# The convolution's diagonals behind the last norm's root in GpSimd's queue, and the lower parts of 5 routing chunks instead of 12 on GpSimd

## The chip, the cores and the metric

The program runs on one core of one Trainium2 chip. The metric is device time in microseconds (us), the median of several runs. "The profile" is one execution recorded by the hardware profiler.

## The reference

Three blocks run one after the other on 256 tokens of width 1024, in float32: an attention layer with a product-key expert network (PEER), a block with a conformer convolution and a recurrent mixer between feed-forward layers, and a block with sliding-window attention. The change touches the PEER network and the convolution:

```python
def peer_ffn(h, w_q, sub_k1, sub_k2, expert_u, expert_v):
    q = (ht @ w_q).reshape(T, 8, 256)
    s1 = einsum('thd,nd->thn', q[..., :128], sub_k1)       # 128 scores per head and half
    s2 = einsum('thd,nd->thn', q[..., 128:], sub_k2)
    v1, i1 = top_k(s1, 16);  v2, i2 = top_k(s2, 16)
    cand = v1[..., :, None] + v2[..., None, :]             # 256 sums per head
    vals, pos = top_k(cand, 16)
    experts = i1 * 128 + i2, taken at pos
    gates = softmax(vals)
    w = gelu(x . expert_u[experts]) * gates
    return sum of w * expert_v[experts]

def conformer_conv_module(x, ...):                         # x is rms_norm of the residual
    a, gate = split(x @ w_in + b_in, 2)
    h = a * sigmoid(gate)
    h = causal depthwise convolution of width 31 of h, + b_dw
    return silu(layer_norm(h)) @ w_out + b_out
```

## The kernel before

**Weights.** Tokens are held as two tiles of 128 rows. Weights come from memory in chunks of 128 x 2048 float32 (1 MB), loaded by SyncE's queue into `raw`, which has three buffers. `stream` splits each chunk in two halves of 1024 columns: ScalarE rounds the high part `wh` (L107), and the lower part `wl` = `raw` - `wh` (L109) is made by VectorE, or by GpSimd where `pool` is true. TensorE multiplies three times: high by high (L125), high by the activations' lower part (L126), lower part by high (L127). `wh` and `wl` have three slots.

```python
eng = nc.gpsimd if pool else nc.vector
for i in range(2):
    nc.scalar.copy(h[:, c], r[:, c])
    eng.tensor_tensor(l[:, c], r[:, c], h[:, c].bitcast(F32), op=OP.subtract)
```

**The PEER network.** Since every expert can be chosen, `up` multiplies all of `peer_u` by the tokens (64 chunks, each with two results that ScalarE turns to `ga` by gelu, L1048), while `routing` finds the chosen experts on VectorE; `weave` alternates steps of the two. For each token tile `routing` forms `cand` (L951) and takes the top 16 of 8 heads (L920 to L923), then the gates: `g` = values minus the largest (L962), the exponent on ScalarE, `den`, `g` (L965 to L967). The positions are split in `xb` (L985). For each half (first key, second key) `ib` (L990) holds the key numbers as float16, `eq` (L993, L995, L997) picks the chosen ones, `idx` (L999) is their sum, which TensorE transposes (L1001). Later the chosen experts are written as one-hot products to memory, from where the down projection reads them. TensorE runs the chunks of `up` while VectorE does all that, and takes one chunk after the other; ScalarE holds `wh` of coming chunks, the exponent and `ga` in one queue. The lower parts of chunks 0 to 11 of `up` are GpSimd's.

**The convolution.** `pre_norm` makes the normed input `xn`: ScalarE squares two halves of the residual into sums (L151), GpSimd adds them (`va`, L155) and takes the root by a power (`ya`, L158) in `rstd`, VectorE multiplies (L173), TensorE transposes (L213), and ScalarE and VectorE split the result (`xx`, L120, L121). This is done for both token tiles, just behind the feed-forward layer before. `conv` then streams `conv_in` (8 chunks, gated to `hp`) and convolves by channel blocks of 128: blocks 0 to 3 and 8 taps of block 5 by chains of multiply-adds on VectorE (L1220, L1224), block 4 on ScalarE and GpSimd (L1240, L1243), blocks 6 and 7 and 23 taps of block 5 by TensorE: for each tap a product with a diagonal matrix (`pc`, L1265). The diagonals `dg` are made from the weights `wd` by 14 `affine_select` instructions on GpSimd (L1213), each of up to 7 taps (128 x 896). Behind the products come transposes (`pt`, L1276), a layer norm and `conv_out`.

**Order.** Each engine takes its instructions in the order of its queue. A scheduling framework lays this order out when the program is built; the code's order goes in, and `issue_after(x)` keeps an instruction behind `x`.

Of the kernel before, what the change touches and what calls it, by code (L numbers as in the profile page):

```python
# [15 lines left out]
OP = mybir.AluOpType  # L16
# [10 lines left out]
class Core:  # L27
# [117 lines left out]
    def rstd(self, parts, n, p=128):  # L145

        nc = self.nc
        ss = self.sm.tile([128, 2], F32, tag="ss", name="ss")[:p]
        for i, part in enumerate(parts):
            junk = self.wk.tile([128, 512], F32, tag="junk", name="junk")[:p, :part.shape[-1]]  # L150
            nc.scalar.activation(junk, part, AF.Square, scale=n ** -0.5, accum_out=ss[:, i:i + 1])  # L151
        v = self.sm.tile([128, 1], F32, tag="va", name="va")[:p]
        y = self.sm.tile([128, 1], F32, tag="ya", name="ya")[:p]
        if len(parts) == 2:
            nc.gpsimd.tensor_scalar(v, ss[:, 0:1], EPS, ss[:, 1:2], op0=OP.add, op1=OP.add)  # L155
        else:
            nc.gpsimd.tensor_scalar(v, ss[:, 0:1], EPS, None, op0=OP.add)
        nc.gpsimd.tensor_tensor(y, v, self.half[:p, 0:1], op=OP.pow)  # L158
        return y

    def halves(self, x, p=128):
# [724 lines left out]
class Peer:  # L886
# [153 lines left out]
    def up(self):  # L1040
        k, nc = self.k, self.k.nc
        for c in range(64):
            hl = k.stream(k.a["peer_u"][c], pool=c < 12)
            for i in range(2):
                ps = k.tp((128, S), tag="tq")
                k.linear_stat(hl, i, ps)
                g = self.pool.tile([128, S], F32, tag="ga", name="ga", bufs=self.AHEAD)
                nc.scalar.activation(g, ps, AF.Gelu_apprx_tanh)  # L1048
                self.ga[c * 2 + i] = g
            yield  # L1050

    def down(self, up):
        k, nc, pool = self.k, self.k.nc, self.rp
        acc = [[k.acc(name=f"o{t}{h}") for h in range(2)] for t in range(2)]
# [14 lines left out]
        for c in range(64):  # L1069
            if c % 4 == 0:  # L1070
                G = pool.tile([128, S // self.GRP, 8, self.GRP], F32, tag="g8", name="G", bufs=2)
                nc.scalar.dma_start(G, self.gd[:, :, c * 2:c * 2 + 8, :])
            for _ in range(1 if c else 5):
                next(up, None)
            vs = [x.rearrange("p (e h n) -> p e h n", e=2, h=2) for x in k.stream(k.a["peer_v"][c])]
            ws = []
            for i in range(2):
                e = c * 2 + i
                w = self.ga.pop(e)
                w3 = w.rearrange("p (a b) -> p a b", b=self.GRP)  # L1080
                nc.vector.tensor_tensor(w3, w3, G[:, :, e % 8, :], op=OP.mult)
                wh = pool.tile([128, S], F32R, tag="wth", name="wth", bufs=5)
                wl = pool.tile([128, S], F32R, tag="wtl", name="wtl", bufs=5)
                k.split(wh, wl, w)
                ws.append((wh, wl))
            if c < 62:
                for i in range(2):
                    part(c * 2 + i, vs, ws[i])
            else:
                last += [(c * 2 + i, vs, ws[i]) for i in range(2)]  # L1090
# [11 lines left out]
    def run(self):  # L1102
        up = self.up()
        done = [0]

        def n(i):
            x = i >= 7 if i < 20 else i % 5 in (0, 3)
            x = min(x, self.AHEAD // 2 - 5 - done[0])
            done[0] += max(x, 0)
            return max(x, 0)  # L1110
        with self.k.tc.tile_pool(name="route", bufs=1) as self.rp:
            weave(self.routing(), up, n)
        with ExitStack() as ctx:
            self.rp = ctx.enter_context(self.k.tc.tile_pool(name="down", bufs=1))
            self.k.work(ctx)
            self.down(up)
# [3 lines left out]
class Block2:  # L1120
# [68 lines left out]
    def conv(self):  # L1189
        k, nc, a = self.k, self.k.nc, self.k.a  # L1190
        with ExitStack() as ctx:
            k.temp(ctx, "cvt")
            pool = ctx.enter_context(k.tc.tile_pool(name="cv", bufs=1))
            tl = lambda n, sh, dt=F32: pool.tile(sh, dt, name=n)
            par, wd = tl("par", [128, 3, 8]), tl("wd", [128, 8, 31])
# [9 lines left out]
            y = hp[:, :, 30:]  # L1205
            ysum, y5 = tl("ysum", [128, S]), tl("y5", [128, S])
            diag = {cb: tl(f"dg{cb}", [128, n, 128]) for cb, n in ((7, 31), (6, 31), (5, first))}
            for cb in (5, 6, 7):
                n = diag[cb].shape[1]
                for w in range(0, n, 7):  # L1210
                    d = diag[cb][:, w:min(w + 7, n)]
                    m = d.shape[1]
                    nc.gpsimd.affine_select(d, wd[:, cb, w:w + m, None].to_broadcast([128, m, 128]), pattern=[[0, m], [-1, 128]],  # L1213
                                            base=0, channel_multiplier=1, compare_op=OP.is_equal, fill=0.0)
            tap = lambda cb, w: hp[:, cb, w:w + S]
            chains = []

# [239 lines left out]
class Block3:  # L1457
# [267 lines left out]
    def mix(self, l, nt):  # L1725
        k, nc, a = self.k, self.k.nc, self.k.a
        with ExitStack() as ctx:
# [16 lines left out]
            def attention():  # L1744
                flush()
                for t in (2, 0, 1)[3 - nt:]:
                    yield from self.attention(l, t, sink, ga)
            side, conv = attention(), self.conv(l, nt)
            weave(iter(lambda: next(conv, True), True), side, lambda i: 2)
            for _ in side:  # L1750
                pass
# [226 lines left out]
```

## Time and profile before

| | |
|---|---|
| median of 3 runs | 2835.39 us (2831.9 to 2836.78) |
| the profiled execution | 2840.85 us, of which the span 2838.9 |
| mean granted TensorE clock | 0.981 of full speed |
| TensorE busy | 2726.2 us, 96% of the span |
| VectorE busy | 1851.3 us, 65% |
| ScalarE busy | 1417.2 us, 50% |
| GpSimd busy | 295.1 us, 10% |

PE is TensorE, DVE VectorE, ACT ScalarE, POOL GpSimd, SP SyncE. L109 is line 109 of the program; `wl<-raw,wh` names what an instruction writes and reads. A row in order of time gives start, duration, engine, line, operation, tiles, shapes and the number of instructions that it sums up; in brackets stands how long the engine stood idle before it, and whose work ended that. The routing stretch is that from 338 to 421 us, and the convolution's norm lies at 1304 to 1326 us.

### The profile page before, as it was taken

Reading aid. Unit: us, or ns where it says so; the run is one execution under the profiler, and the core shown is the slowest. Engines: PE = TensorE matmul, PEld = TensorE weight load, DVE = VectorE, ACT = ScalarE, POOL = GpSimd, SP = SyncE. Lnnn points to the kernel's source line nnn. Section 1 sums busy time; section 2 is a strip of 40 time slices with the busy share of each in tenths; the row PEclk is TensorE's granted clock in tenths of the full one; section 3 lists DMA queues with packets and bytes.
Section 4 is the critical chain, followed back from the end, with each engine's and each line's share of the span. In section 5 each row is a group of like instructions: output and inputs, shape, how many; then the busy total and the mean of one; then the engine's idle time right before and its main releaser. Section 6 shows DMA issues by size and latency. Waiting matters only on the chain.

```text
span 2838.9 us, 42369 instructions
## 1 busy us (share of the span) xinstructions
PE 2726.2 (96%) x16916; PEld 2423.5 (85%) x16916; DVE 1851.3 (65%) x3170; ACT 1417.2 (50%) x2454; POOL 295.1 (10%) x314
## 2 busy tenths in 40 slices
PE   7899979999999999999999999999999999999999
PEld 5787979989999887888888888897888878889897
DVE  6757698775555555766876576676766565466654
ACT  5544445544444555654556455524655454454543
POOL 2001650000000000002400000151001110000100
PEclk9899989999999999999999999999999999999999
DMA  5323436796665555554255465524554334433452
GB/s 208 146 103 140 145 125 249 287 314 220 208 216 202 191 193 205 193 191 167 76 199 193 170 215 188 195 90 155 195 192 158 121 115 156 163 131 123 162 193 104
DMA packets 105973, 496.58 MB, mean 175 GB/s; under 512 B 11040, under 2 KB 44320, under 8 KB 50224
## 3 DMA queue, kind: packets, MB, share of 16 engines
q1 hardware_dynamic: 61632, 443.15, 43.8%
q10 hardware_dynamic: 44144, 50.74, 5.4%
q8 instruction: 132, 2.16, 0.3%
q14 instruction: 65, 0.53, 0.1%
HBM read 476.03 MB, written 17.83 MB: 174 GB/s over the span
## 4 chain that ended last, share of the span: by engine, by line
PE 61%; issue 23%; DVE 8%; POOL 3%; ACT 3%; DMA 2%; ACTq 0%; POOLq 0%; DVEq 0%
PE acc L288 5%; PE tp L127 4%; PE tp L126 4%; PE tp L125 4%; PE o L1065 4%; PE o L1064 4%; PE o L1067 4%; PE acc L125 4%; PE acc L127 4%; PE acc L126 3%; PE acc L290 2%; PE o L342 2%; PE o L343 2%; PE o L345 2%; DVE wl L109 2%
## 5 line engine op out<-in xcount | busy, mean ns | idle before, releaser
L109 DVE TENSOR_TENSOR wl<-raw,wh 128x1024 fp32r<-128x1024 f32 x808 | 965.6, 1224 | 432.0 <-ACT wh L107 426.4
L107 ACT CAST wh<-raw 128x1024 fp32r<-128x1024 f32 x848 | 855.9, 1044 | 508.2 <-PE tp L126 136.2
L125 PE MATMUL tp<-xx,wh 128*128 128x256 f32 (+1 forms) x1440 | 410.0, 285 | 5.3 <-ACT ga L1048 5.3
L288 PE MATMUL acc<-xx,wh 128*128 128x512 f32 x1216 | 414.0, 393 | 0.0
L127 PE MATMUL tp<-xx,wl 128*128 128x256 f32 (+1 forms) x1440 | 410.3, 285 | 2.2 <-DVE wl L109 2.1
L126 PE MATMUL tp<-xx,wh 128*128 128x256 f32 (+1 forms) x1440 | 411.1, 285 | 0.0
L290 PE MATMUL acc<-xx,wl 128*128 128x256 f32 x1064 | 298.1, 280 | 0.0
L125 PEld LDWEIGHTS tp<-xx,wh 128*128 128x128 f32 x1440 | 275.1, 191 | 8.8 <-ACT ga L1048 5.7
L127 PEld LDWEIGHTS tp<-xx,wl 128*128 128x128 f32 x1440 | 275.2, 191 | 2.7 <-DVE wl L109 2.6
L126 PEld LDWEIGHTS tp<-xx,wh 128*128 128x128 f32 x1440 | 273.8, 190 | 2.3
L288 PEld LDWEIGHTS acc<-xx,wh 128*128 128x128 f32 x1216 | 218.7, 188 | 39.3
L125 PE MATMUL acc<-wh,xx 128*128 128x256 f32 (+2 forms) x672 | 225.3, 336 | 2.6 <-ACT xx L120 2.2
L126 PE MATMUL acc<-wl,xx 128*128 128x256 f32 (+2 forms) x672 | 220.9, 330 | 5.2 <-DVE wl L109 5.2
L155 POOL TENSOR_SCALAR va<-ss 128x1 f32<-128x1 f32 (+1 forms) x49 | 24.2, 495 | 1940.2 <-ACT junk L151 1759.5
L127 PE MATMUL acc<-wh,xx 128*128 128x256 f32 (+2 forms) x672 | 219.5, 329 | 2.8 <-DVE xx L121 2.7
L290 PEld LDWEIGHTS acc<-xx,wl 128*128 128x128 f32 x1064 | 200.1, 188 | 5.6
L1065 PE MATMUL o<-wl,wth 128*128 128x512 f32 x512 | 200.5, 392 | 3.0 <-DVE wl L109 2.9
L1064 PE MATMUL o<-wh,wth 128*128 128x512 f32 x512 | 200.6, 392 | 0.0
L1067 PE MATMUL o<-wh,wtl 128*128 128x512 f32 x512 | 159.5, 390 | 0.0
L126 PEld LDWEIGHTS acc<-wl,xx 128*128 128x128 f32 x672 | 130.5, 194 | 16.3 <-DVE wl L109 6.9
L1182 DVE TENSOR_TENSOR u<-acc,u 128x256 f32<-128x256 f32 x152 | 64.1, 422 | 122.3 <-ACT u L1181 122.3
L127 PEld LDWEIGHTS acc<-wh,xx 128*128 128x128 f32 x672 | 129.3, 193 | 15.8 <-DVE xx L121 5.3
(518 smaller groups left out, 5264.3 us busy)
## 6 DMA issues: line engine op xcount, KB each, us to landing
raw<-in_ffn_in_dram SPq DMA_DIRECT2D x88, 1024.0 KB, 4.8
raw<-in_peer_u_dram SPq DMA_DIRECT2D x64, 1024.0 KB, 4.9
raw<-in_peer_v_dram SPq DMA_DIRECT2D x64, 1024.0 KB, 4.8
raw<-in_ffn_out_dram SPq DMA_DIRECT2D x44, 1024.0 KB, 4.8
raw<-in_w_up_dram SPq DMA_DIRECT2D x32, 1024.0 KB, 4.8
raw<-in_w_down_dram SPq DMA_DIRECT2D x32, 1024.0 KB, 4.8
gd<-gt ACTq DMA_DIRECT2D x16, 1024.0 KB, 6.0
G<-gd ACTq DMA_DIRECT2D x16, 1024.0 KB, 7.0
```

Source lines behind the costliest of these rows:

```text
L107: nc.scalar.copy(h[:, c], r[:, c])
L109: eng.tensor_tensor(l[:, c], r[:, c], h[:, c].bitcast(F32), op=OP.subtract)
L125: mm(out, ah, bh, start=start, stop=False)
L126: mm(out, ah, bl, start=False, stop=False)
L127: mm(out, al, bh, start=False, stop=stop)
L288: self.nc.tensor.matmul(ps, h[:, kb], self.xx[:, :, kb, :S], start=kb == 0, stop=kb == 7)
L290: self.nc.tensor.matmul(ps[:, 0], l[:, kb], self.xh[:, kb, :S], start=False, stop=False)
L342: mm(acc[t][h], hi[:, k, ts], wv[0][:, h], start=st, stop=False)
L1064: mm(acc[t][h], wh, vh[:, h], start=st, stop=False)
L1065: mm(acc[t][h], wh, vl[:, h], start=False, stop=False)
L1067: mm(acc[t][h], wl, vh[:, h], start=False, stop=sp)
L1182: nc.vector.tensor_tensor(u, ps[:, 0], u, op=OP.add)
```

## The change

The root's instruction is kept as `k.root`. The 14 selects are held behind it; `rstd` runs for every norm, and at this place the last one is that of the second token tile ahead of the convolution. In `up` the lower parts of chunks 3 to 6 and 9 to 11 go from GpSimd to VectorE; chunks 0, 1, 2, 7 and 8 stay on GpSimd. Lines from 1214 on move by one.

```diff
@@ rstd
-        nc.gpsimd.tensor_tensor(y, v, self.half[:p, 0:1], op=OP.pow)
+        self.root = nc.gpsimd.tensor_tensor(y, v, self.half[:p, 0:1], op=OP.pow)
         return y
@@ Peer.up
         for c in range(64):
-            hl = k.stream(k.a["peer_u"][c], pool=c < 12)
+            hl = k.stream(k.a["peer_u"][c], pool=c in (0, 1, 2, 7, 8))
@@ Block2.conv
                     m = d.shape[1]
-                    nc.gpsimd.affine_select(d, wd[:, cb, w:w + m, None].to_broadcast([128, m, 128]), pattern=[[0, m], [-1, 128]],
-                                            base=0, channel_multiplier=1, compare_op=OP.is_equal, fill=0.0)
+                    with k.tc.issue_after(k.root.ins):
+                        nc.gpsimd.affine_select(d, wd[:, cb, w:w + m, None].to_broadcast([128, m, 128]), pattern=[[0, m], [-1, 128]],
+                                                base=0, channel_multiplier=1, compare_op=OP.is_equal, fill=0.0)
```

In the following rows - is the order before, + that of the change, and x3 three such rows in sequence. The first place is GpSimd's queue at the norm ahead of the convolution (`va` and `ya` belong to the root, `dg` are the diagonals):

```order
-L1213 AFFINE_SELECT dg_12908<-wd 128x896 x3
-L155 TENSOR_SCALAR va<-ss 128x1
-L1213 AFFINE_SELECT dg_12908<-wd 128x256
-L158 TENSOR_TENSOR ya<-va,half 128x1
-L1213 AFFINE_SELECT dg_12907<-wd 128x896 x4
-L1213 AFFINE_SELECT dg_12907<-wd 128x384
-L1213 AFFINE_SELECT dg_12906<-wd 128x896 x4
-L1213 AFFINE_SELECT dg_12906<-wd 128x384
+L155 TENSOR_SCALAR va<-ss 128x1
+L158 TENSOR_TENSOR ya<-va,half 128x1
+L1214 AFFINE_SELECT dg_12908<-wd 128x896 x3
+L1214 AFFINE_SELECT dg_12908<-wd 128x256
```

Both halves of the root now stand ahead of all selects.

The second place is VectorE's queue at the end of the first token tile's top 16, just ahead of `g`:

```order
 L923 MAX_INDEX pos<-val,mr 128x8
 L921 MATCH_REPLACE mr<-val,cand 128x112
-L990 CAST ib<-i_2476 128x128
+L109 TENSOR_TENSOR wl<-raw,wh 128x1024
 L922 MAX val<-mr 128x8
-L990 CAST ib<-i_2477 128x128
+L109 TENSOR_TENSOR wl<-raw,wh 128x1024
 L923 MAX_INDEX pos<-val,mr 128x8
 L962 TENSOR_TENSOR g<-val 128x128
```

Two lower parts, those of chunk 3, now stand in the top 16, and the two `ib` stand later.

The third place is VectorE's queue some twenty rows later, where the first `idx` is made:

```order
 L995 TENSOR_TENSOR eq<-eq,ib 128x2048
+L109 TENSOR_TENSOR wl<-raw,wh 128x1024
+L997 TENSOR_TENSOR eq<-eq 128x1024
+L109 TENSOR_TENSOR wl<-raw,wh 128x1024
+L997 TENSOR_TENSOR eq<-eq 128x512
+L990 CAST ib<-i_2477 128x128
+L997 TENSOR_TENSOR eq<-eq 128x256
 L993 TENSOR_TENSOR eq<-xb,iota 128x2048
+L999 TENSOR_TENSOR idx<-eq 128x128
+L995 TENSOR_TENSOR eq<-eq,ib 128x2048
```

Lower parts of chunks 4 and 5 now stand between the steps of `eq`; four more (chunks 5 and 6) follow in the steps of the second `eq`, ahead of the second `idx`. At the second token tile chunks 9 to 11 stand in the same places. SyncE's queue keeps its order.

## Rows read from the trace of the kernel before

**Rows 1.** The page's first part: busy time, share of the span and instructions of each engine.

```profile
PE 2726.2 (96%) x16916; PEld 2423.5 (85%) x16916; DVE 1851.3 (65%) x3170; ACT 1417.2 (50%) x2454; POOL 295.1 (10%) x314
```

**Rows 2.** TensorE in order of time in the routing stretch, the four instructions ahead of which it stood idle for longest.

```profile
362.28 0.39 PE L125 MATMUL tp<-xx,wh 128*128 128x256 f32 x1 [2.70 <-ACT ga L1048]
...
376.10 0.45 PE L1001 MATMUL tp<-ident,idx 128*128 128x128 f32 x1 [7.30 <-DVE idx L999]
...
393.27 0.38 PE L125 MATMUL tp<-xx,wh 128*128 128x256 f32 x1 [2.63 <-ACT ga L1048]
...
414.71 0.47 PE L1001 MATMUL tp<-ident,idx 128*128 128x128 f32 x1 [2.61 <-DVE idx L999]
```

**Rows 3.** Busy time in the routing stretch. Columns: length; busy time with instructions of PE, PEld (TensorE's weight loads), DVE, ACT, POOL; granted clock; DMA share; GB/s.

```profile
338.00:421.00 83.00, 67.75 (x517) 66.96 (x516) 82.93 (x277) 34.90 (x53) 48.28 (x20) 0.90 0.38 133
```

**Rows 4.** The same view for the stretch behind each of the four stops.

```profile
362.28:368.00 5.72, 5.72 (x35) 5.72 (x36) 5.69 (x3) 2.49 (x4) 5.54 (x3) 0.70 0.53 186
376.10:380.00 3.90, 3.90 (x19) 3.90 (x20) 3.90 (x24) 2.14 (x5) 0.76 (x1) 0.50 0.01 2
393.27:398.00 4.73, 4.73 (x27) 4.73 (x28) 4.73 (x8) 2.16 (x4) 3.77 (x2) 0.64 0.35 147
414.71:418.00 3.29, 3.29 (x17) 3.29 (x18) 3.29 (x7) 1.21 (x2) 0.00 (x0) 0.57 0.92 311
```

**Rows 5.** GpSimd in order of time in the routing stretch, two runs of lower parts.

```profile
360.61 7.36 POOL L109 TENSOR_TENSOR wl<-raw,wh 128x1024 fp32r<-128x1024 f32 x3 [3.21 <-ACT wh L107]
...
401.83 11.87 POOL L109 TENSOR_TENSOR wl<-raw,wh 128x1024 fp32r<-128x1024 f32 x4 [2.79 <-ACT wh L107]
```

**Rows 6.** VectorE in order of time in the routing stretch.

```profile
346.73 2.21 DVE L951 TENSOR_TENSOR cand<-v,v 128x512 f32<-128x512 f32 x1
...
360.90 2.34 DVE L985 TENSOR_TENSOR xb<-x,y 128x128 f16<-128x128 f32 x1
...
365.63 3.42 DVE L993 TENSOR_TENSOR eq<-xb,iota 128x2048 f16<-128x2048 f16 x1
...
369.98 0.28 DVE L985 TENSOR_TENSOR xb<-x,y 128x128 f16<-128x128 f32 x1
370.19 1.22 DVE L995 TENSOR_TENSOR eq<-eq,ib 128x2048 f16<-128x2048 f16 x1
371.32 1.22 DVE L993 TENSOR_TENSOR eq<-xb,iota 128x2048 f16<-128x2048 f16 x1
...
376.07 0.68 DVE L951 TENSOR_TENSOR cand<-v,v 128x512 f32<-128x512 f32 x1
...
402.18 3.42 DVE L993 TENSOR_TENSOR eq<-xb,iota 128x2048 f16<-128x2048 f16 x1
...
408.07 3.41 DVE L995 TENSOR_TENSOR eq<-eq,ib 128x2048 f16<-128x2048 f16 x1
411.41 3.05 DVE L997 TENSOR_TENSOR eq<-eq 128x256 f16<-128x256 f16 x2
```

**Rows 7.** The convolution's norm and stage: instructions of GpSimd, VectorE, ScalarE and TensorE in order of time; the row at 1364.71 is from the chain that ended last (start, duration, engine, tile, line, instructions); the last row is busy time, columns as in rows 3.

```profile
1304.45 0.36 POOL L155 TENSOR_SCALAR va<-ss 128x1 f32<-128x1 f32 x1 [2.46 <-ACT junk L151]
...
1305.49 0.88 DVE L173 TENSOR_SCALAR xn<-xn,ya 128x512 f32<-128x512 f32 x2 [0.85 <-POOL ya L158]
...
1313.38 0.19 ACT L151 ACTIVATION_READ_ACCUMULATOR junk<-X 128x1 f32 x1
...
1314.86 2.85 POOL L1213 TENSOR_SCALAR_AFFINE_SELECT dg<-wd 128x896 f32<-128x896 f32 x3 [3.66 <-DMA wd<-in_conv_dw_dram]
...
1315.05 0.28 PE L127 MATMUL acc<-wh,xx 128*128 128x256 f32 x1
...
1317.81 0.30 POOL L155 TENSOR_SCALAR va<-ss 128x1 f32<-128x1 f32 x1
...
1319.15 2.31 DVE L173 TENSOR_SCALAR xn<-xn,ya 128x512 f32<-128x512 f32 x2 [5.30 <-POOL ya L158]
...
1320.40 2.23 PE L213 MATMUL tp<-ident,xn 128*128 128x128 f32 x8 [5.07 <-DVE xn L173]
...
1323.90 10.14 DVE L109 TENSOR_TENSOR wl<-raw,wh 128x1024 fp32r<-128x1024 f32 x6
...
1364.71 36.71 PE pc L1265 x170
...
1397.68 0.48 DVE L1224 SCALAR_TENSOR_TENSOR hp<-hp,wd,ya 128x256 f32<-128x256 f32 x1
...
1320.40:1326.00 5.60, 5.60 (x26) 4.94 (x27) 4.46 (x5) 3.34 (x5) 5.60 (x6) 0.55 0.00 0
```

**Rows 8.** ScalarE and VectorE in order of time in and behind the routing stretch, and, last, the line that issues the loads of the raw weights, within 300 to 440 us: from issue to landing.

```profile
348.18 1.05 ACT L107 CAST wh<-raw 128x1024 fp32r<-128x1024 f32 x1 [2.38 <-PE tp L126]
...
353.86 1.05 ACT L107 CAST wh<-raw 128x1024 fp32r<-128x1024 f32 x1 [2.38 <-PE tp L126]
...
358.18 0.26 DVE L990 CAST ib<-i 128x128 f16<-128x128 uint32 x1
...
358.98 0.27 DVE L962 TENSOR_TENSOR g<-val 128x128 f32<-128x128 f32 x1
...
420.73 3.51 DVE L109 TENSOR_TENSOR wl<-raw,wh 128x1024 fp32r<-128x1024 f32 x3
...
DMA to landing us min/median/max: 4.7/4.8/6.1
```

## The prediction

> **What bounds the kernel now.** I began with the profile's page: TensorE is busy for 96% of the span [rows 1]. Only time in which TensorE stands still or runs at its lower clock can be won, so the next view was TensorE's instructions in order of time, read for their idle notes, in the two stretches that the change touches.
>
> In the routing stretch (338 to 421 us) TensorE stands still four times, for 2.70, 7.30, 2.63 and 2.61 us, 15.24 in all [rows 2]. Two of these wait for `idx`, which VectorE makes, and two for `ga`, which ScalarE writes late because its table for the softmax's exponent waits for VectorE's `g`. VectorE is busy for 82.93 of these 83.00 us [rows 3]; it is the engine that is waited for. After each of the four stops the granted clock is at its lower level for a while: 0.70 over 5.72 us, 0.50 over 3.90, 0.64 over 4.73, 0.57 over 3.29 [rows 4]. The part of full speed that is missing is 1.72 + 1.95 + 1.70 + 1.41 = 6.8 us. **So the most this stretch can give is 15.2 + 6.8 = 22.0 us.**
>
> Why VectorE is late is seen where its rows lie beside GpSimd's. GpSimd's lower parts take about 2.4 us each (three in 7.36, four in 11.87 where VectorE's instructions come between) [rows 5]. While one runs, `xb` takes 2.34 us where it takes 0.28 alone, `eq` 3.42 and 3.41 where it takes 1.22, `cand` 2.21 where it takes 0.68 [rows 6]. The extra time is what was left of GpSimd's instruction. Between 346.73 and 411.41 twelve VectorE instructions stand so, first and last in the rows; at the five differences shown (1.53, 2.06, 2.20, 2.20, 2.19, mean 2.0) that is about 25 us. The top-16 instructions are not stretched.
>
> In the convolution TensorE stands still for 5.07 us at 1320.40, for `xn`, and then runs at 0.55 for 5.60 us, which loses 2.5 [rows 7]: **7.6 us at most.** GpSimd's root is the reason. The sums are read at 1313.57, but the root's first half stands at 1317.81, behind three diagonal selects that began at 1314.86 when their weights had landed [rows 7].
>
> **Part one, the convolution.** The selects now follow the root. In the norm just before, the root's first instruction starts at 1304.45, right after its sums, and `xn` 1.04 later [rows 7]. From 1313.57 that gives 1313.66 and `xn` at 1314.70, where it was 1319.15. Its first half is ready at 1315.15; the second meets the first select (0.95, a third of 2.85) and is ready at 1316.6. TensorE's last matmul ends at 1315.33, so it waits some 0.8 between the halves instead of 5.07 for the first. At full clock it then does by about 1319.4 what took until 1326.0 (5.60 x 0.55 = 3.1 us of work, 0.8 of waiting, 0.2 of slack): 6.6 us earlier.
>
> What waits behind the root now? All fourteen selects, some 12 us of GpSimd's time, and then the lower parts that it makes of this stage's later chunks. The diagonals are wanted at 1364.71 [rows 7], so the selects themselves are covered by more than 30 us.
>
> Does the gain last to the stage's end? TensorE ends its products at 1401.42 (1364.71 + 36.71), and VectorE's chain of taps ends at 1398.16 [rows 7], so the chain may gain 3.3 us less than TensorE before it is waited for. VectorE's first splits, six in 10.14 us against 6 x 1.14 = 6.8 undisturbed [rows 7, 8], lost 3.4 to the selects. They now start about 5.6 earlier, with as many selects beside them. If they lose the same 3.4, the chain ends at 1392.6, before the products' 1394.8. I take 6.0, a little under 6.6. Bounds: 3.3 (the chain gains nothing) and 7.6.
>
> **Part two, the routing.** Fourteen lower parts (chunks 3 to 6 and 9 to 11) go to VectorE at 1.14 each, the spacing in a row of three [rows 8]: 15.9 us more. Eight collisions or so leave, 16 us; four GpSimd instructions (chunks 7 and 8) stay and keep theirs. VectorE's load is the same; what can be won comes from where its work stands. So I walk the new order:
>
> - Chunk 3. ScalarE's casts that take over a slot tell when TensorE leaves a chunk: 348.18 and 353.86, so 5.68 a chunk, and chunk 3 starts at 353.86 [rows 8]. Its first lower part stands where `ib` stood at 358.18, 1.53 earlier as `cand` is no longer stretched: 356.65 to 357.8. TensorE can do two matmuls (0.24), then waits 3.7 us: **a new wait**, with a clock loss of 1.7 (mean of [rows 4]).
> - Chunk 4. VectorE comes to `g` at 359.4 (before: 358.98), so the exponent no longer stops TensorE, which is slowed anyway. `xb`, `eq` and the rest at undisturbed length bring chunk 4's first lower part to 366.4; TensorE is there at 357.8 + 5.68 + 1.7 + 0.5 = 365.7. Wait 0.7. The first `idx` is ready at 370.1; its transpose stands behind 36 of chunk 4's 48 matmuls in the changed program (0.118 each: 370.6), so the 7.30 goes.
> - Chunk 5. Ready at 372.4, TensorE there at 372.1: 0.3.
> - Second `idx`. Undisturbed it is ready at 377.3, after chunk 6's lower parts; TensorE wants it behind 42 of chunk 5's 48 matmuls, at 372.4 + 42 x 0.118 = 377.4. But chunk 7's load goes out when chunk 4's raw tile is free (368.1), lands 4.8 later [rows 8], is cast by 373.9, and GpSimd's two instructions then alternate with VectorE's as they did in the 11.87 us row. That makes it 382. The wait lies between 0 and 4.6; I take 4.0, near the upper end, since the rows show alternation; clock 1.7.
>
> What remains is 3.7 + 1.7 + 0.7 + 0.3 + 4.0 + 1.7 = 12.1 us. The later waits of before (exponent and `idx` of the second token tile) fall away, since TensorE is held up earlier and VectorE has the top-16 of that tile alone. **Routing: 22.0 - 12.1 = 9.9 us.** Bounds: 22.0, and 0.8, if chunk 8 collides too (4.8) and the second exponent wait stays (2.63 + 1.70).
>
> From there to the convolution, and behind it, every engine has its old order, and a TensorE that is busy 96% moves forward as a whole.
>
> **Sum.** 9.9 + 6.0 = 15.9 us off the profiled execution's 2840.85: 2824.95. The median of the runs shown, 2835.39, lies 5.46 below that execution, so **2819.5 us**.
>
> **Rivals.**
> - The new waits eat the routing's gain (chunk 3 and the second `idx` cost as much as the four old stops). For it: VectorE's load does not fall. Against: two of the old stops go in any order. Then 6.0 remain: 2829.4. Chance 0.15.
> - VectorE's chain becomes the convolution's bound. If each of the six splits waits for a whole select, 6 x 0.95 = 5.7 us instead of 3.4, the chain ends at 1394.9, level with the products, and whatever VectorE loses beyond that counts, down to a gain of 3.3: 2823.2. Against: the row shows 3.4. Chance 0.09. The Trainium skill has such a rule ("SBUF — State Buffer", section "Who interferes with whom"): a VectorE instruction with two SBUF inputs and a GpSimd instruction that reads SBUF shut each other out for the whole instruction. The 10.14 us row agrees that they disturb each other and shows less than that full price.
> - Both stretches give all they can, 29.6: 2805.8. Chance 0.06. Against it speaks chunk 3's place behind the top-16.
> - No change: the routing's new waits cost 6 us more than its old stops, as much as the convolution gains: 2835.4. Chance 0.07.
> - Slower: VectorE pays the 15.9 us and gets little back, because chunks 7 and 8 on GpSimd catch as many of its instructions as twelve chunks did. Every stop of TensorE in the routing waits for VectorE, so with x us given back the time changes by 15.9 - x - 6.0; slower than the bound from x below 4, and at x = 0 the time is 2845.3. Against: only four of the eighteen GpSimd instructions of chunks 3 to 11 remain. Chance 0.05.
>
> **Chances.** The forecast has 0.58. A difference under 0.2% (5.7 us) can't be told from none. Faster: 0.58 + 0.15 + 0.09 + 0.06 = 0.88; same 0.07; slower 0.05. The range leaves out the last three cases (0.18): 2809 to 2830.
>
> **What would show it.** In the changed profile: `xn` starts within 1.2 us of the sums' end, and the 5.07 us stop at TensorE is under 2; the selects stand behind the root. VectorE's chain of taps ends before the products. In the routing TensorE has one stop of 3 to 5 us for `wl` at chunk 3 and one for the second `idx`, with clock rows near 0.5 behind both, and no 7.30. The prediction is wrong if stops of TensorE in the routing add up to more than 15 us, if a stop appears at the transposes behind the products, or if the one-hot products (from 440 us on) begin to wait for VectorE.

## The result and the profile after

The changed kernel takes 2819.14 us (median of 9 runs, 2812.40 to 2830.19) against 2836.78 (9 runs, 2831.90 to 2842.31) before: ratio 0.9936, 95% interval 0.9924 to 0.9948. The forecast was 2819.5. The profiled execution takes 2823.47 us, its span is 2821.5, so it lies 17.4 us under that of before.

How much of this each place gave is read from TensorE, which is the engine that must not wait. First the routing: the last score product (L938) lies ahead of it and the first one-hot product (L1033) behind it. Kernel before, TensorE's instructions of these lines (columns: shortest/median/longest in ns, then start of the first and of the last):

```profile
L938 PE MATMUL tp<-keys,qpT x64: 271/275/377, 297.4 to 337.1; 128*128 128x128 f32 x64
...
L1033 PE MATMUL tp<-A,B x512: 217/218/330, 433.4 to 542.4; 128*128 128x128 f16 x171
```

The changed kernel, same lines:

```profile
L938 PE MATMUL tp<-keys,qpT x64: 271/275/377, 294.1 to 333.8; 128*128 128x128 f32 x64
...
L1033 PE MATMUL tp<-A,B x512: 217/218/233, 419.7 to 527.3; 128*128 128x128 f16 x171
```

From 337.1 to 433.4 it is 96.3 us before, from 333.8 to 419.7 it is 85.9 after: **the routing gives 10.4 us.** All times of the changed kernel here lie 3.3 us earlier than those of before; where they are compared, that is taken off.

The convolution: TensorE's last matmul ahead of the transposes, the transposes, and (last row, from the chain that ended last) the diagonals' products. The changed kernel:

```profile
1298.57 0.28 PE L127 MATMUL acc<-wh,xx 128*128 128x256 f32 x1
1299.56 0.66 PE L213 MATMUL tp<-ident,xn 128*128 128x128 f32 x4 [0.71 <-DVE xn L173]
...
1300.68 0.66 PE L213 MATMUL tp<-ident,xn 128*128 128x128 f32 x4 [0.46 <-DVE xn L173]
...
1342.68 36.71 PE pc L1266 x170
```

From 1298.57 to 1342.68 it is 44.11 us; before it was 1364.71 - 1315.05 = 49.66 [rows 7]. **The convolution gives 5.55 us.** Together 15.95; the remaining 1.4 us of the two executions' difference are a net of larger ones in stretches that the change does not touch: 3.3 us gained ahead of the routing, 2.8 between the two places, and 4.6 lost behind the convolution.

The routing's stops after, TensorE in order of time (the stop of 7.30 is gone, [rows 2] had four):

```profile
354.62 0.39 PE L127 MATMUL tp<-xx,wl 128*128 128x256 f32 x1 [3.81 <-DVE wl L109]
...
386.06 0.40 PE L125 MATMUL tp<-xx,wh 128*128 128x256 f32 x1 [2.40 <-ACT ga L1048]
...
402.26 0.33 PE L1001 MATMUL tp<-ident,idx 128*128 128x128 f32 x1 [0.21 <-DVE idx L999]
```

With three more of 0.24, 0.33 and 0.24 they add up to 7.23 us, where before it was 15.24. Busy time from the last score product to the first one-hot product, in the kernel before and in the changed one, and of the pieces behind the two stops in the changed kernel (columns as in rows 3):

```profile
337.07:433.41 96.34, 81.09 (x629) 80.26 (x628) 90.36 (x284) 41.48 (x65) 49.21 (x20) 0.91 0.40 142
...
333.76:419.69 85.93, 78.70 (x629) 77.41 (x628) 84.47 (x298) 41.72 (x65) 17.24 (x6) 0.96 0.43 158
...
354.62:358.00 3.38, 3.38 (x19) 3.38 (x20) 3.38 (x17) 1.59 (x2) 0.00 (x0) 0.64 0.24 63
...
386.06:390.00 3.94, 3.94 (x20) 3.94 (x21) 3.94 (x16) 2.45 (x3) 0.00 (x0) 0.57 0.76 302
```

TensorE does the same number of instructions here with 8.0 us less of standing still and 2.4 less of busy time; its clock is granted at 0.96 (0.91 before). VectorE is still busy for 84.47 of the 85.93 us, but that is 5.9 us less than before, although it has fourteen instructions more.

**Chunk 3, as forecast.** VectorE at the end of the first top 16 (rows of the top 16 between them are left out):

```profile
353.33 1.24 DVE L109 TENSOR_TENSOR wl<-raw,wh 128x1024 fp32r<-128x1024 f32 x1
...
354.64 1.23 DVE L109 TENSOR_TENSOR wl<-raw,wh 128x1024 fp32r<-128x1024 f32 x1
...
356.03 0.29 DVE L962 TENSOR_TENSOR g<-val 128x128 f32<-128x128 f32 x1
```

TensorE goes on at 354.62, when the first of these is done.

**Chunk 7, not as forecast.** GpSimd in order of time, from two stretches that overlap: its first lower part alone, and the first two together.

```profile
370.87 6.58 POOL L109 TENSOR_TENSOR wl<-raw,wh 128x1024 fp32r<-128x1024 f32 x1 [33.54 <-ACT wh L107]
...
370.87 8.94 POOL L109 TENSOR_TENSOR wl<-raw,wh 128x1024 fp32r<-128x1024 f32 x2 [33.54 <-ACT wh L107]
```

VectorE beside them:

```profile
371.16 1.22 DVE L109 TENSOR_TENSOR wl<-raw,wh 128x1024 fp32r<-128x1024 f32 x1
...
372.50 1.22 DVE L109 TENSOR_TENSOR wl<-raw,wh 128x1024 fp32r<-128x1024 f32 x1
373.63 0.28 DVE L999 TENSOR_TENSOR idx<-eq 128x128 f32<-128x128 f16 x1
...
374.91 0.26 DVE L990 CAST ib<-i 128x128 f16<-128x128 uint32 x1
...
375.64 1.89 DVE L1009 CAST gT<-res 128x128 f16<-128x128 f32 x1
...
377.72 2.24 DVE L1010 TENSOR_TENSOR gT<-res,gT 128x128 f16<-128x128 f32 x1
```

While VectorE does one TENSOR_TENSOR behind another (lower parts, `eq`, `idx`, `cand`, up to 375), it is not stretched at all and GpSimd stands aside: 6.58 us for an instruction that takes 2.4 alone. This instruction ends at 377.45, 2.5 us behind the start of `ib`, the first VectorE instruction that is no TENSOR_TENSOR; so it got through when that row had ended. Only from `gT` on is VectorE stretched again. So the second `idx` is ready at 373.91 and no stop is left there. The price comes later. SyncE in order of time, and ScalarE:

```profile
379.84 0.33 SPq L116 DMA_DIRECT2D raw<-in_peer_u_dram  x1
```

```profile
378.01 0.39 ACT L1048 ACTIVATE ga<-tp 128x256 f32<-128x256 f32 x1
384.68 1.04 ACT L107 CAST wh<-raw 128x1024 fp32r<-128x1024 f32 x1 [6.28 <-DVE val L919]
385.63 0.38 ACT L1048 ACTIVATE ga<-tp 128x256 f32<-128x256 f32 x1
```

SyncE issues the load of chunk 9 at 379.84, as soon as GpSimd's second lower part of chunk 7 has ended at 379.81 (370.87 + 8.94). Chunk 6's buffer had been free since 373.7 (372.50 + 1.22), but the changed program gives chunk 9 the buffer of chunk 7, and chunk 10 that of chunk 6; so chunk 9's load waits for GpSimd. The load lands 4.7 us later, at 384.5; the cast follows at 384.68. The row names VectorE's `val` as the releaser, but the cast reads nothing of it; the load ended last. TensorE's `ga` stands behind this cast in ScalarE's queue: that is the stop of 2.40.

### The profile page after: what moved, and what is told of

It is laid out like the page before. It is cut to its first block, busy times and chain, and to the rows that moved or that the text cites. A ratio compares the mean times of both kernels' runs of the same rounds, so it can differ in the third digit from the quotient of the medians.

```text
span 2821.5 us, 42371 instructions
## 1 busy us (share of the span) xinstructions
PE 2720.2 (96%) x16916; PEld 2416.3 (86%) x16916; DVE 1845.4 (65%) x3184; ACT 1417.3 (50%) x2454; POOL 267.2 (9%) x300
## 4 chain that ended last, share of the span: by engine, by line
PE 61%; issue 23%; DVE 7%; POOL 3%; ACT 3%; DMA 2%; ACTq 0%; POOLq 0%; DVEq 0%; SPq 0%
PE acc L288 5%; PE tp L127 4%; PE tp L125 4%; PE tp L126 4%; PE o L1065 4%; PE o L1064 4%; PE o L1067 4%; PE acc L125 3%; PE acc L127 3%; PE acc L126 3%; PE acc L290 2%; DVE wl L109 2%; PE o L342 2%; PE o L345 2%; PE o L343 2%
## 5 line engine op out<-in xcount | busy, mean ns | idle before, releaser
L109 DVE TENSOR_TENSOR wl<-raw,wh 128x1024 fp32r<-128x1024 f32 x822 | 982.9, 1223 | 428.6 <-ACT wh L107 423.1
L126 PEld LDWEIGHTS acc<-wl,xx 128*128 128x128 f32 x672 | 130.2, 194 | 16.7 <-DVE wl L109 7.4
```

The costliest lines, as they stand in the source:

```text
L126: mm(out, ah, bl, start=False, stop=False)
```

## The experiments

"Path" below is the time from the last score product to the first one-hot product (96.3 us before, 85.9 in the changed kernel). The seven runs were compared with the kernel before on the chip on which they ran.

**1. The selects alone.** The changed kernel, with the lower parts as before:

```diff
-            hl = k.stream(k.a["peer_u"][c], pool=c in (0, 1, 2, 7, 8))
+            hl = k.stream(k.a["peer_u"][c], pool=c < 12)
```

> The selects behind the root, all twelve chunks' lower parts left on GpSimd. Theory (the two parts add up, each with its own stop of TensorE): in the trace the stop of 5.07 us for xn ahead of the convolution is under 2 us in several pieces, the routing keeps its four stops of about 2.7, 7.3, 2.6 and 2.6 us, and the time is 5 to 6 us under the kernel before (ratio 0.998). Rival one (the gain is given back behind the convolution, where TensorE waits for the next norms): TensorE is 5.5 us ahead at the transposes behind the diagonals' products, but less than 2 us ahead of the kernel before 100 us later, and the ratio is 0.9995 or more. Rival two (VectorE's chain of taps sets the stage's end): a new stop of 2 to 3 us at the transposes behind the products, gain 3.3 us.

Measured: ratio 0.9978 (0.9963 to 0.9992), that is 6.2 us of the 2839.95 of before. TensorE ahead of the convolution:

```profile
1308.78 0.28 PE L127 MATMUL acc<-wh,xx 128*128 128x256 f32 x1
1308.96 0.66 PE L213 MATMUL tp<-ident,xn 128*128 128x128 f32 x4
...
1310.08 0.66 PE L213 MATMUL tp<-ident,xn 128*128 128x128 f32 x4 [0.46 <-DVE xn L173]
...
1352.05 36.71 PE pc L1266 x170
```

From 1308.78 to 1352.05 it is 43.27 us, 6.4 less than before. The path through the routing is 95.6, and its stops are the four old ones (2.70, 7.32, 2.93, 2.64). No stop at the transposes behind the products is longer than before, so rival two falls.

Behind the convolution this execution does lose 3.1 us against that of before, from the first product of the diagonals to the first product of line 1375, which is 1376 where the selects were moved:

```profile
L1266 PE MATMUL pc<-hp,dg x170: 377/378/381, 1351.9 to 1388.4; 128*128 128x256 f32 x170
...
L1376 PE MATMUL tp<-qq,kd x224: 217/275/294, 1836.5 to 1907.0; 128*128 128x64 f32 x112
```

1836.5 - 1351.9 = 484.6 us, where it was 481.5 before (1364.5 to 1846.0). But the next experiment, which leaves the convolution as it was, shows the same 484.5; and experiment 6, with the selects moved, shows 481.6 (1340.2 to 1821.8). So it is no price of the selects, and rival one falls too. The gain ahead of the products repeats: in the other kernels with the moved selects (experiments 3, 4, 6 and 7) the same stretch is 5.6 to 6.4 us shorter than before.

**2. The lower parts alone.** The kernel before, with one line changed:

```diff
-            hl = k.stream(k.a["peer_u"][c], pool=c < 12)
+            hl = k.stream(k.a["peer_u"][c], pool=c in (0, 1, 2, 7, 8))
```

> Lower parts of chunks 0, 1, 2, 7 and 8 alone on GpSimd, the selects as in the kernel before. Theory (the routing's part is worth what its stops say): stops of TensorE in the routing of 3.8 us for wl at chunk 3 and 2.4 us for ga at chunk 8's end, no stop over 1 us for idx, the convolution keeps its 5.07 us stop; about 10 us under the kernel before (ratio 0.9965). Rival (part of the changed kernel's lead is scatter between executions, as its 3.3 us lead before the routing begins suggests): the two parts alone give clearly less than the changed kernel, together under 13 us.

Measured: ratio 0.9963 (0.9949 to 0.9977), 10.5 us. The path is 424.7 - 338.8 = 85.9, the stops are 3.77 for `wl` at chunk 3 and 2.42 for `ga`, none for `idx`; ahead of the convolution TensorE stands for 5.44 us (5.07 before). GpSimd's first lower part of chunk 7 stands aside here as well:

```profile
375.94 6.52 POOL L109 TENSOR_TENSOR wl<-raw,wh 128x1024 fp32r<-128x1024 f32 x1 [33.57 <-ACT wh L107]
```

And behind the convolution, with the old selects:

```profile
L1265 PE MATMUL pc<-hp,dg x170: 377/378/381, 1349.7 to 1386.2; 128*128 128x256 f32 x170
...
L1375 PE MATMUL tp<-qq,kd x224: 217/275/294, 1834.2 to 1904.6; 128*128 128x64 f32 x112
```

The two parts add up: 6.2 + 10.5 = 16.7 us of about 2840, and 0.64% for both is 18.2, within the intervals. The rival falls.

**3. Chunks 7 and 8 on VectorE too.** The changed kernel, with

```diff
-            hl = k.stream(k.a["peer_u"][c], pool=c in (0, 1, 2, 7, 8))
+            hl = k.stream(k.a["peer_u"][c], pool=c < 3)
```

> The changed kernel with the lower parts of chunks 7 and 8 on VectorE too, so that GpSimd makes those of chunks 0 to 2 only. Theory (the 2.40 us stop for ga is chunk 9's raw load, which SyncE issues only when GpSimd's lower parts of chunk 7 are done, 6.58 us for the first because VectorE streams beside it): the stop is gone or under 1 us, no VectorE instruction between 370 and 385 us is stretched (gT 0.3 instead of 1.9 and 2.2), and VectorE's 4 x 1.14 = 4.6 us more are largely paid by 3.6 us of stretching that go: 2 to 4 us under the changed kernel (about 2816). Rival (the stop is the second exponent's, that is VectorE's load ahead of the second g): g comes 1 us later or more, the stop for ga grows to 3 us or more, and the time is that of the changed kernel or above.

Measured: 2818.78 us, ratio 0.9929 (0.9907 to 0.9951), which this many runs can't tell from the changed kernel's 0.9936. The trace tells the cause apart. TensorE's longest stops:

```profile
355.23 0.38 PE L127 MATMUL tp<-xx,wl 128*128 128x256 f32 x1 [3.77 <-DVE wl L109]
...
387.81 0.39 PE L127 MATMUL tp<-xx,wl 128*128 128x256 f32 x1 [0.46 <-DVE wl L109]
...
403.57 0.33 PE L1001 MATMUL tp<-ident,idx 128*128 128x128 f32 x1 [1.33 <-DVE idx L999]
```

VectorE's `gT` and the second `g`:

```profile
376.65 0.22 DVE L1009 CAST gT<-res 128x128 f16<-128x128 f32 x1
...
376.97 0.27 DVE L1010 TENSOR_TENSOR gT<-res,gT 128x128 f16<-128x128 f32 x1
...
389.22 0.30 DVE L962 TENSOR_TENSOR g<-val 128x128 f32<-128x128 f32 x1
```

The stop for `ga` is gone, `gT` takes 0.22 and 0.27, and the second `g` stands 54.8 us behind the last score product (334.4), where the changed kernel has 390.38 - 333.8 = 56.6: it comes earlier although VectorE has two lower parts more ahead of it (the four of chunks 7 and 8, where the changed kernel has two of chunk 9). The load of chunk 9 goes out at 374.35 here, with the end of chunk 6's last lower part (374.32). So the stop of 2.40 was the held-up load and not VectorE's work; the rival falls. A stop of 1.33 for the fourth `idx` takes part of it back: the path is 83.8, which is 2.1 less than in the changed kernel. The 2 to 4 us expected of the time are not shown.

**4. Chunk 3 on GpSimd as well.** The changed kernel, with

```diff
-            hl = k.stream(k.a["peer_u"][c], pool=c in (0, 1, 2, 7, 8))
+            hl = k.stream(k.a["peer_u"][c], pool=c in (0, 1, 2, 3, 7, 8))
```

> The changed kernel with chunk 3's lower parts on GpSimd as well (0 to 3, 7 and 8). Theory (chunk 3's wait of 3.81 us is a matter of place in VectorE's queue alone: its wh is there at 341.5 us, GpSimd stands idle from 337 to 371, and the top 16 beside it is not stretched): no stop for wl at chunk 3, cand 2.2 us instead of 0.7 once, the 2.40 us stop for ga stays; 3 to 5 us under the changed kernel (about 2815). Rival (VectorE's chain from the top 16 to idx is what TensorE waits for in any order, chunk 3 only shows it first): a stop of 2 to 5 us appears later, for wl of chunk 4 or 5 or for idx, and the time is within 2 us of the changed kernel.

Measured: 2823.09 us, ratio 0.9943 (0.9927 to 0.9960): not faster. Here the rival holds for the time and in that a stop appears later; it is another stop than the rival named, though. TensorE's stops:

```profile
358.85 0.40 PE L125 MATMUL tp<-xx,wh 128*128 128x256 f32 x1 [2.71 <-ACT ga L1048]
...
367.29 0.30 PE L1001 MATMUL tp<-ident,idx 128*128 128x128 f32 x1 [0.89 <-DVE idx L999]
...
368.24 0.39 PE L125 MATMUL tp<-xx,wh 128*128 128x256 f32 x1 [0.52 <-ACT ga L1048]
...
385.87 0.39 PE L125 MATMUL tp<-xx,wh 128*128 128x256 f32 x1 [1.18 <-ACT ga L1048]
...
394.48 0.39 PE L125 MATMUL tp<-xx,wh 128*128 128x256 f32 x1 [2.68 <-ACT ga L1048]
```

Chunk 3's stop is gone, and the exponent's stop of the kernel before [rows 2] is back at 358.85 with its old length (2.71), as is that of the second tile at 394.48 (2.68); the stop of 2.40 is 1.18. With one more of 0.20 the stops add up to 8.18, the path is 86.8. **The 3.8 us at chunk 3 stand ahead of the exponent's stop and pay for it:** TensorE, held up there, no longer reaches `ga` before the exponent is done. GpSimd's first instruction of chunk 7 takes 9.17 us here.

**5. GpSimd's lower parts in smaller pieces.** The kernel before, with

```diff
-                eng.tensor_tensor(l[:, c], r[:, c], h[:, c].bitcast(F32), op=OP.subtract)
+                for q in ([slice(c.start + x, c.start + x + n // 8) for x in range(0, n // 2, n // 8)] if pool else [c]):
+                    eng.tensor_tensor(l[:, q], r[:, q], h[:, q].bitcast(F32), op=OP.subtract)
```

> The kernel before, with each of GpSimd's lower parts cut into four pieces of 256 columns; same work, same engines. Theory (a VectorE instruction with two inputs waits for what is left of the GpSimd instruction that is running, no longer): xb, eq and cand that took 2.2 to 3.4 us in the routing take at most some 0.7 us more than alone (xb under 1.0, eq under 2.0), but more of them are stretched; TensorE's stop for the first idx, 7.3 us, shrinks to 4 to 6. Rival (VectorE stands back until GpSimd has no more work of this kind): xb and eq keep 2 us and more of extra time, and the stop for idx stays at 7 us.

Measured: ratio 0.9984 (0.9972 to 0.9997). VectorE in the routing (lines moved by one):

```profile
356.72 0.70 DVE L986 TENSOR_TENSOR xb<-x,y 128x128 f16<-128x128 f32 x1
...
358.01 1.77 DVE L994 TENSOR_TENSOR eq<-xb,iota 128x2048 f16<-128x2048 f16 x1
...
362.67 1.76 DVE L996 TENSOR_TENSOR eq<-eq,ib 128x2048 f16<-128x2048 f16 x1
```

TensorE's stop for an `idx` of the second tile:

```profile
407.88 0.48 PE L1002 MATMUL tp<-ident,idx 128*128 128x128 f32 x1 [4.47 <-DVE idx L1000]
```

`xb` takes 0.70 and `eq` 1.77, where it was 2.34 and 3.42 [rows 6]: a stretched instruction waits for what is left of one GpSimd instruction, and the rival falls. But more of them are stretched, 44 in the path instead of 12 (counted where a duration lies over 0.25 us above the shortest of its kind), by 22.7 us in all instead of 25.1. The stop for the first `idx` is 6.64, not the 4 to 6 expected, and one of 4.47 stands at the second tile, where it was 2.61: smaller pieces spread the price and lower it little. The path is 94.6, 1.7 less than before.

**6. No lower part of these chunks on GpSimd.** The changed kernel, with

```diff
-            hl = k.stream(k.a["peer_u"][c], pool=c in (0, 1, 2, 7, 8))
+            hl = k.stream(k.a["peer_u"][c], pool=False)
```

> The changed kernel with all lower parts of the up chunks on VectorE, those of chunks 0 to 2 too. Theory (beside the top 16 GpSimd's lower parts stretch nothing, so those of chunks 0 to 2 are free help, and taking them away costs VectorE 6 x 1.14 = 6.8 us ahead of the first g): stops of TensorE in the routing grow by 3 to 7 us over those with chunks 0 to 2 on GpSimd (6.4 us), time 2 to 6 us above that kernel, 2821 to 2825. Rival (GpSimd's lower parts cost VectorE what they save it everywhere): no more stops than with chunks 0 to 2, time within 1 us of 2818.8.

Measured: 2820.77 us, ratio 0.9935 (0.9919 to 0.9952), not to be told from experiment 3. Stops are 7.08, 0.7 more than there, where 3 to 7 had been expected; the path is 84.9, 1.1 more. So neither the theory nor its rival describes it. The reason is seen ahead of the routing (columns as in rows 3):

```profile
320.00:338.00 18.00, 18.00 (x153) 17.82 (x152) 17.75 (x88) 8.90 (x15) 0.00 (x0) 1.00 0.51 188
```

VectorE is busy for 17.75 us of these 18; in the changed kernel it is 13.14, in experiment 3 12.50. Most of the six lower parts filled time in which VectorE had stood idle. The first three chunks on GpSimd are worth about 1 us of the path, not 6.8.

**7. Transposes and exponent later.** Chunks 0 to 2 on GpSimd; `idx` in two buffers; both transposes of `idx` behind the last matmul issued so far, with a step of the chunks ahead of them, then the exponent:

```diff
+            def soft(it):
+                with k.tc.issue_after(it.ins): nc.scalar.activation(g, g, AF.Exp)
+                ...  # den, g as before
+            for j in range(2):
+                pt = k.tp((128, 128), tag="tp")
+                with k.tc.issue_after(k.mm.ins): nc.tensor.transpose(pt, ids[j], k.ident)
+                it = nc.scalar.copy(self.iT[j][:, t * 128:(t + 1) * 128], pt)
+            soft(it); yield
```

> Lower parts of chunks 0 to 2 on GpSimd; besides, both transposes of idx stand one chunk later in TensorE's queue, and the exponent with den and g behind them in ScalarE's and VectorE's. Theory (what is left in the routing, beside chunk 3's 3.8 us, is TensorE and ScalarE reaching an instruction early that nobody needs soon, and not VectorE's load): no stop over 0.5 us for idx or ga, chunk 3's stop stays, stops in all under 5 us; 1 to 4 us under the kernel with chunks 0 to 2 alone (about 2816). Rival (VectorE is the bound in this stretch: what TensorE doesn't wait for idx it waits for wl): a stop of 1 to 4 us for wl at chunks 4 to 11, stops in all 6 us or more, time as before that edit.

Measured: 2816.39 us, ratio 0.9924 (0.9904 to 0.9943). The new place of the transposes does what the theory says of `idx` and `ga`, and none of the stops for `wl` appears that the rival names; but the stops in all are not under 5. Stops for `idx` are gone, the longest for `ga` is 0.24, chunk 3's 3.78 stays, and a new one of 1.78 appears at the transposition of `g`, which now comes late:

```profile
426.64 0.30 PE L1007 MATMUL tp<-ident,g 128*128 128x128 f32 x1 [1.78 <-DVE g L967]
```

Stops add up to 5.80, 0.6 less than in experiment 3. Since the one-hot products stand at other places of TensorE's queue here, the path is taken to the last product of `wh` in the down projection instead (its start minus that of the last score product): 1104.5 - 338.2 = 766.3, with 1100.4 - 334.4 = 766.0 in experiment 3 and 780.2 before. The edit gives nothing that could be measured. Neither version is shown to be faster than the changed kernel; both are faster than the kernel before.

## Why the prediction was right, step by step

- **The root.** Forecast: `xn` 1.2 us behind the sums, the stop under 2. The sums are read at 1297.07, `xn` starts at 1298.22; stops of 0.71 and 0.46, and one of 0.47 behind them. The granted clock is 1.00 from 1299.56 to 1305 us. The convolution gives 5.55 us in this execution and 6.4 in experiment 1, for 6.0.
- **VectorE's splits and chain.** Forecast: the same loss of 3.4 us to the selects, the chain ahead of the products by 2.2. The changed kernel's rows:

```profile
1302.60 10.34 DVE L109 TENSOR_TENSOR wl<-raw,wh 128x1024 fp32r<-128x1024 f32 x6
...
1375.96 0.48 DVE L1225 SCALAR_TENSOR_TENSOR hp<-hp,wd,ya 128x256 f32<-128x256 f32 x1
```

  10.34 for six is a loss of 3.5 (10.14 - 6 x 1.14 = 3.3 before, which the forecast gives as 3.4); the chain ends at 1376.44, the products at 1379.39, 2.95 later. The rival that the chain becomes the bound falls; its time should have been 2835.39 - 9.9 - 3.3 = 2822.2, not 2823.2.
- **VectorE's load.** Forecast: eight stretched instructions fewer, 16 us, against 15.9 us more of lower parts, so the load stays the same. Measured in the path: stretched instructions fall from twelve to the two of `gT`, by 21.5 us (25.1 to 3.6), and VectorE's busy time from 90.36 to 84.47. This term was put too low, since the four instructions left on GpSimd catch two of VectorE's and not four.
- **The exponent's wait.** The forecast says that ScalarE's table waits for `g`. In the trace before, the table is loaded at 355.21 without waiting; it is the exponent that waits for `g` (2.79 us, to 359.28), and behind it the gelu's table is loaded anew (1.28 us) ahead of `ga`. The sum does not hang on this.
- **Chunk 3.** Forecast: first lower part at 356.65, a wait of 3.7, clock loss 1.7. Measured: 353.33 (with the 3.3 us: 356.6), 3.81, and 0.36 x 3.38 = 1.2.
- **Chunks 4 and 5, first `idx`.** Forecast: waits of 0.7 and 0.3, `idx` at 370.1. Measured: 0.24 + 0.33 and 0.24; `idx` at 366.89, with the 3.3 us 370.2.
- **The second `idx`: the step that failed.** It was put at 382, because GpSimd's instructions would alternate with VectorE's as in the 11.87 us row [rows 5]; the wait was taken at 4.0 and 1.7. It was ready at 373.91, with the 3.3 us at 377.2: the undisturbed 377.3. GpSimd stood aside, and the lower end of the range given for this wait, 0, was the right one.
- **"The later waits fall away": failed too.** The stop for the second `ga` is there, 2.40 and 0.43 x 3.94 = 1.7 of clock. Its cause is not the exponent, as it was before, but chunk 9's load behind GpSimd's lengthened instruction (experiment 3).

The last two errors are of one size, 5.7 us too much and 4.1 too little. That the routing came to 10.4 where 9.9 was forecast rests in part on this, and is luck to that extent: less standing still was to give 6.5 us (15.24 - 8.7) and gave 8.0, the clock was to give 3.4 (6.8 - 3.4) and TensorE's busy time fell by 2.4. Luck is also in the median: 2819.14 lies 0.4 from the forecast, but 17.6 below the median of before that was measured beside it, where 15.9 was forecast; no run shows where the other 1.7 come from. The rest of the sum was right for the reasons given: the walk through VectorE's new order with undisturbed durations hit the ready times that it names for lower parts and `idx` within 0.2 us, since GpSimd did not stretch them.

Of the rivals, "the new waits eat the gain" is seen in small at chunk 3, where a new wait stands in place of the exponent's. "Both stretches give all they can" would have needed chunk 3's wait to go without another one coming; experiment 4 shows another coming. "VectorE gets little back" falls with the changed kernel itself: VectorE got 21.5 us back for the 15.9 that it paid.

## What to carry to other kernels

Look in a helper engine's queue for what stands ahead of a tiny instruction on the critical path: here 3 us of preparation, wanted 50 us later, cost 6. A stop that is removed is only won if the next one is not already waiting behind it; walk the waited engine's queue with undisturbed durations and see what comes late next. And when a helper engine shares its work with a busy one, count what its delay holds up (a buffer, and the load that needs it), not only what it stretches.

## What the runs showed of the hardware

- Which of GpSimd and VectorE stands aside is not always the same. Where GpSimd's instruction ran first, VectorE's waited for its rest (2.0 us of 2.4; 0.5 of 0.74 with smaller pieces, experiment 5). At chunk 7, where VectorE did one TENSOR_TENSOR behind another, GpSimd's waited: 6.58, 6.52 and 9.17 us in three kernels for an instruction of 2.4, and each time it ended 2.5 us behind the start of the first VectorE instruction of another kind. The Trainium skill ("SBUF — State Buffer", section "Who interferes with whom") says that the one that issues first keeps the shared ports for the whole instruction and the other is shut out; the rows agree where GpSimd's instruction came first. They do not agree at chunk 7: by its row GpSimd's instruction started at 370.87, ahead of VectorE's at 371.16 and 372.50, and still it was the one that waited. Nor does a row of TENSOR_TENSORs always keep GpSimd out: in the kernel before it came in between them (four in 11.87 us, beside `eq` of 3.42 [rows 5, 6]), and in the convolution its selects did (six lower parts in 10.34 us). What decides between the two was not settled.
- Two executions differ by several us in stretches whose order is the same: from the first product of line 1375 (1376 in experiments 4 and 6) to the end of the span it is 992.6 us in experiment 6 and 999.3 in experiment 4. Stops of TensorE of the same kind are alike within 0.4 us from run to run (3.81, 3.77, 3.77, 3.78 at chunk 3; 5.07 and 5.44 at the norm), so a cause of 2 us was told apart in the traces where the times could not.
